# Hybrid decoder step on one core: block transposes on VectorE with transfers for the spatial branch's v and the second half's x, and sample products in pairs

## The chip, the cores and the metric

The kernel runs on one core of one Trainium2 chip. A core has TensorE for matrix products (PE in the views, its weight loads PEld), VectorE (DVE), ScalarE (ACT), GpSimd (POOL), SyncE (SP), whose queue issues this kernel's transfers, and 16 DMA engines that carry them. The metric is the time of one execution in microseconds (us); lower is better.

## The reference, cut to what matters

The reference is one step of a one-layer decoder with two gated branches, in float32. The same weights serve a prompt of 2048 tokens and a sample group of 8 sequences with 4 tokens each; the model width is 1024.

```python
h = layernorm(x) * (1 + scale) + shift
u_a, v_a, z_a, qkv, z_b, b_raw, a_raw, ga, gb = split(h @ w_in)        # 9232 columns
# spatial branch: chunks of 128 tokens, 8 heads of 128 channels
vn = layernorm(gelu(v_a)) * lnv_g + lnv_b                                # over the channels of a token
s  = einsum('hts,bnshc->bnthc', tril(w_s), vn) + b_s
y_a = gelu(u_a) * s * silu(z_a)
# recurrent branch: short convolution of q, k, v, then the gated delta rule per head
S_t = a_t S_{t-1} + beta_t k_t (v_t - a_t S_{t-1}^T k_t)^T;  o_t = S_t^T q_t
y_b = rmsnorm(o) * silu(z_b)
m   = sigmoid(ga) * (y_a @ w_pa) + sigmoid(gb) * (y_b @ w_pb)
x_new = layernorm(ALPHA * x + gate * (m @ w_o)) * ln_g + ln_b
```

For the sample group each of the 8 sequences starts from its own 128x128 state per head, so the products with the state are 8 separate ones per head, each for 4 tokens.

## The kernel before, in words

The prompt is worked in two halves of 1024 tokens; the 32 sample tokens ride with the first half. Activations lie with channels on the partitions and tokens along the free axis. A projection (`project`) makes 128 output channels at a time, a "group": for each of 8 slices of the input channels three fp32r products of a high and a low part, over column groups of 384, 384 and 256+32 tokens in the first half and 512 and 512 in the second. A group's weights are two transfers of 256 KB into `raw` buffers (three of them), which ScalarE and VectorE split into high and low parts in one of two `TWHL` buffers (`wload`). What becomes of a product is a "sink".

The order of all instructions is not written by hand. Parts of the work are generators that name an engine, an estimated duration and what they depend on; `Sched.run` advances its own model of the engines and always emits the instruction whose modelled start (plus a priority term) is earliest. Each engine and the one DMA queue on SP then run their instructions in that fixed order. Buffers are named roles over shared units (`Rc`, `Yc`), taken with `("a", role)` and given back with `S.release`; a generator that finds none free waits.

The order of the stages in each half: the heads of the recurrent branch (q, k, v, z_b and some of ga, per head), the gb groups, the v groups of the spatial branch, its u and z groups with the gating products, the rest of ga, then `w_pa`, `w_pb` and `w_o`. In the first half, beginning with the first gb group, a background task `h_next_all` prepares the second half's input, chunk after chunk.

Three places are touched:

- `v_sink` (line 1776), first half only. The v projection leaves channels on the partitions; the layer norm of v needs tokens there. A sink applies gelu (into a buffer of role `og`, four of them), TensorE transposes each 128x128 chunk (`tp`, line 450, a product with the identity) into a PSUM bank, and ScalarE copies the bank into the token-major buffers `("vt", c)`. After the eighth group `v_norm` normalises each chunk and stores it in `d_vh`; `vh_load` brings it back per head for the gating products in `gate`. In the second half v is projected token-major (`v_tokens`) and not transposed.
- `h_next` (line 801). For each of the 8 chunks of the second half: load x, normalise, 8 transposes of 128x128 on TensorE, then the affine with `scale` and `shift` on 128x128 pieces out of PSUM, four on ScalarE and four on VectorE, and two transfers of 256 KB into `d_h`, channel-major. `h_tiles` (line 836) loads the eight 128x1024 tiles of `d_h` near the end of the first half and splits each into the `X` buffers of the second half as these come free.
- `sample_head` (line 1644), once per head in the first half. Eight products of 128x64 weights (`kx`, zero outside one sequence's tokens) with that sequence's state (128x128) accumulate in one PSUM bank. Later two products with 32 rows, 128 output channels and 512 columns (`kp` with `xe`) add the new outer products to the state. Both are plain float32, and the trace shows two TensorE instructions for each such product.

The convolution's v (`v_token`, line 1346) is already turned by VectorE in 32x32 blocks (`vtrans`, line 426) and four transfers of 128-byte runs into a DRAM scratch `d_v`, and comes back token-major.

Of the kernel before, what the change touches and what calls it, by code (L numbers as in the profile page):

```python
# [11 lines left out]
ALU = mybir.AluOpType  # L12
# [3 lines left out]
KT = 8  # L16
# [153 lines left out]
def hybrid_step_kernel(ctx: ExitStack, tc: tile.TileContext, x_prompt, x_sample, state_conv, state_ssm,  # L170
# [97 lines left out]
    role("og", [Yc(28, 1), Yc(29, 1), Yc(30, 1), Yc(31, 1)])  # L268
# [21 lines left out]
    role("hf", [Yc(2, 1), Yc(3, 1), Yc(6, 1), Yc(7, 1)])  # L290
# [55 lines left out]
    d_vh = dram("d_vh", 9 * P * D)  # L346
    d_gb = dram("d_gb", KT * P * TW)
# [174 lines left out]
    def init_small():  # L522
# [8 lines left out]
        S.signal("small", t)  # L531

# [268 lines left out]
    def h_next(c):  # L801

        yield from x_norm(1, c, "hb")
        xb, t0 = S.ev[("xn", 1, c)]
        e = 0.0
        for i in range(2):
            pb = yield ("a", "pt")
            t = t0
            for k in range(4):
                t = yield from tp(Q(pb[0], k * P, P), V(xb[0] + (4 * i + k) * P, P), dep=max(t, pb[2]))  # L810
            fb = yield ("a", "hf")
            tg = max(t, fb[2])
            for k in range(4):
                t = yield from affine(V(fb[0] + k * P, P), Q(pb[0], k * P, P), 4 * i + k, k < 2, tg)
                e = max(e, t)
            S.release(pb, e)
            t = yield from dma(DV(d_h, 4 * i * P * HALF + c * P, [HALF, P], [P * HALF, 4], [1, P]),
                               V(fb[0], [P, 4], [1, P]), dep=e)
            S.release(fb, t)
            S.signal(("hB", c, i), t + 500)  # L820
        S.release(xb, e)

    def h_next_all():
        for c in range(8):
            S.spawn(h_next(c), 2.0)
            if c:
                yield ("w", ("hB", c - 1, 1))
# [8 lines left out]
    def h_tiles(todo, role, after):  # L836
        if after is not None:
            yield ("w", after)
        while todo:
# [6 lines left out]
            for c in range(8):  # L846
                t = max(t, (yield ("w", ("hB", c, k // 4))))
            t = yield from dma(V(b[0], HALF), DV(d_h, k * P * HALF, [HALF, P], [1, HALF]), dep=max(t, b[2]))
            t = max(t, (yield ("w", ("Xfree", 1, k))))
# [794 lines left out]
    def sample_head(h):  # L1644
        me = hd(0, h)
        t = 0.0
        for s in range(3):
# [30 lines left out]
        es, npq, am, m2, us = x + 320, x + 352, x + 416, x + 448, x + 480  # L1678
# [10 lines left out]
        t = yield from act(V(am, NS, **k32), Q(pb[0], 64, NS, **k32))  # L1689
# [3 lines left out]
        t = yield from tt(V(us, NS, **k32), V(m2, NS, **k32), Q(pb[0], 128, NS, **k32), ALU.subtract)  # L1693
# [16 lines left out]
        rb = yield ("a", "Rb")  # L1710
        t = yield from stt(V(rb[0], P, **k32), Q(pb[0], 0, P, **k32), V(c_sneg + h, 1, **k32), V(vs, P, **k32),
                           ALU.mult, ALU.add, dep=max(t4, t, rb[2]))
# [3 lines left out]
        S.release(pb, max(t, t5))  # L1716
        pb = yield ("a", "pt")
        t = yield from mm(Q(pb[0], 0, P, **k32), V(us, NS, **k32), V(rb[0], P, **k32), dep=max(t, pb[2]))
        t = yield from act(V(rb[0], P, **k32), Q(pb[0], 0, P, **k32))
# [14 lines left out]
        ys = x + 448  # L1734
# [9 lines left out]
        for i in range(2):  # L1744
            xe = yield ("a", "kx")
            t1 = yield from tt(V(xe[0], [P, 4], [1, P], **k32), bc(V(rb[0], P, **k32).unsqueeze(1), [NS, 4, P]),
                               bc(V(c_sel + 4 * i, 4, **k32).unsqueeze(2), [NS, 4, P]), ALU.mult, dep=max(tx, xe[2]))
            pb = yield ("a", "pt")
            t = yield from mm(Q(pb[0], 0, 512), V(kp, P, **k32), V(xe[0], 512, **k32), dep=max(t1, pb[2]))
            S.release(xe, t)  # L1750
            a = V(sb0[0] + 512 * i, 512)
            t = yield from tt(a, a, Q(pb[0], 0, 512), ALU.add, dep=max(t, t2))
            S.release(pb, t)
# [22 lines left out]
    def v_sink(half, g):  # L1776
        def sink(cgi, pb, t):
# [5 lines left out]
            cs = chunks(half, cgi)  # L1783
            ta = 0.0
            for c in cs + ([8] if ns_ else []):
                if (half, c) not in vtok and g == 0:
                    vtok[half, c] = None
                    vtok[half, c] = yield ("a", ("vt", c))
                    S.signal(("vt", half, c), vtok[half, c][2])
                ta = max(ta, (yield ("w", ("vt", half, c))))  # L1790
# [525 lines left out]
```

## Time and profile before

| what | us |
|---|---|
| three runs | 2719.08, 2724.36, 2723.06 |
| median | 2723.06 |
| the profiled execution | 2721.62 |
| its span, first to last instruction | 2719.9 |
| TensorE busy in it | 2676.6 |
| VectorE busy | 1467.0 |
| ScalarE busy | 1002.8 |
| GpSimd busy | 557.0 |

The span is what the trace covers; the execution's own time is 1.7 us more. The mean granted TensorE clock was 0.997 of the full one. Matmuls overlap in the pipeline, so the time that one costs is read from the starts of its neighbours and not from its own duration.

### The profile page before, as it was taken

To read this page: it belongs to the slowest core of one execution; us is meant where nothing else is said; L and a number is where in the kernel's file an instruction comes from. 1 tells how busy PE (TensorE), PEld (TensorE's weight loads), DVE (VectorE), ACT (ScalarE), POOL (GpSimd) and SP (SyncE) were. 2 spreads that over 40 slices of the span, in tenths; PEclk is the share of its full clock that TensorE was granted. 3 is DMA by queue.
4 is the path that set the end of the run, shared out by engine and by line. 5 is a ranking of instruction groups with operands and counts; after the bars stand their busy time and mean duration, and the time that the engine had idled before them with its cause. 6 is when DMAs were issued, how large, how long until landed. Compare 5 with 4: busy or idle time off the path is not lost.

```text
span 2719.9 us, 44021 instructions
## 1 busy us (share of the span) xinstructions
PE 2676.6 (98%) x16386; PEld 2351.3 (86%) x16386; DVE 1467.0 (54%) x3234; ACT 1002.8 (37%) x2710; POOL 557.0 (20%) x1452
## 2 busy tenths in 40 slices
PE   6999999999999999999999999999999999999998
PEld 3989999999899999999997888888888888888876
DVE  5677667777652353433547666666662323433446
ACT  5544444545343222221224535344542312222120
POOL 2044544324400000000000443433351000000001
PEclk9999999999999999999999999999999999999999
DMA  6232333223463232332433333333332422233332
GB/s 214 68 95 78 90 105 91 72 70 101 141 211 95 64 115 76 94 105 91 140 109 101 96 97 81 85 93 78 84 86 83 125 99 76 72 112 104 108 121 85
DMA packets 445618, 272.70 MB, mean 100 GB/s; under 512 B 141530, under 2 KB 411154, under 8 KB 445403
## 3 DMA queue, kind: packets, MB, share of 16 engines
q1 hardware_dynamic: 445402, 269.89, 34.6%
q8 instruction: 128, 2.10, 0.3%
q14 instruction: 88, 0.71, 0.1%
HBM read 205.70 MB, written 64.10 MB: 99 GB/s over the span
## 4 chain that ended last, share of the span: by engine, by line
PE 95%; DMA 2%; DVE 1%; ACT 1%; issue 0%; SPq 0%; POOL 0%; POOLq 0%; ACTq 0%; DVEq 0%
PE psum L447 90%; PE psum L452 3%; DMA arena<-in_w_o_dram 0%; ACT arena L398 0%; DMA arena<-in_w_in_dram 0%; PE psum L1483 0%; PE psum L1509 0%; PE psum L1520 0%; DVE arena L730 0%; DMA arena<-in_state_ssm_dram 0%; DVE arena L732 0%; PE psum L1489 0%; DVE arena L423 0%; PE psum L650 0%; DMA Y0F<-in_x_prompt_dram 0%
## 5 line engine op out<-in xcount | busy, mean ns | idle before, releaser
L447 PE MATMUL psum<-TX,TWHL 128*128 128x384 f32 (+3 forms) x9296 | 1973.4, 360 | 3.8 <-DVE TX L407 3.4
L447 PEld LDWEIGHTS psum<-TX,TWHL 128*128 128x128 f32 (+1 forms) x9296 | 1554.6, 188 | 164.0 <-issue 10.6
L398 ACT ACTIVATE arena<-psum 128x128 bf16<-128x128 f32 (+10 forms) x920 | 311.8, 348 | 769.9 <-PE psum L447 587.9
L436 POOL TENSOR_TENSOR arena<-arena 128x4 f32<-128x4 f32 (+4 forms) x139 | 120.1, 865 | 1598.3 <-DVE arena L417 1388.7
L423 DVE SCALAR_TENSOR_TENSOR arena<-arena 128x512 f32<-128x512 f32 (+8 forms) x625 | 345.8, 563 | 95.3 <-ACT arena L398 84.9
L410 POOL TENSOR_TENSOR arena<-arena 128x60 f32<-128x60 f32 (+24 forms) x992 | 358.6, 361 | 169.6 <-DMA d_v<-arena 57.5
L407 DVE TENSOR_TENSOR TWHL<-arena,TWHL 128x512 fp32r<-128x512 f32 (+1 forms) x344 | 233.1, 685 | 240.9 <-ACT TWHL L398 238.7
L423 DVE SCALAR_TENSOR_TENSOR arena<-arena,psum 128x128 f32<-128x128 f32 (+3 forms) x342 | 132.2, 403 | 360.3 <-PE psum L447 249.9
L398 ACT ACTIVATE TWHL<-arena 128x512 fp32r<-128x512 f32 x344 | 214.3, 627 | 219.1 <-PE psum L447 103.4
L398 ACT ACTIVATE arena<-arena 128x128 f32<-128x128 f32 (+9 forms) x509 | 229.4, 486 | 118.2 <-DVE arena L423 81.8
L407 DVE TENSOR_TENSOR arena<-arena 128x1024 f32<-128x1024 f32 (+13 forms) x259 | 114.3, 446 | 15.0 <-DMA arena<-in_lnv_g_dram 4.9
L447 PE MATMUL psum<-arena 128*128 128x128 f32 (+8 forms) x524 | 102.3, 293 | 1.2 <-ACT arena L398 1.0
L452 PE MATMUL psum<-arena 128*128 128x128 f32 (+7 forms) x381 | 93.2, 269 | 3.4 <-ACT TX L398 1.5
L423 DVE SCALAR_TENSOR_TENSOR arena<-psum,arena 128x512 f32<-128x512 f32 (+4 forms) x80 | 39.8, 509 | 103.8 <-PE psum L447 103.8
L447 PEld LDWEIGHTS psum<-arena 128*128 128x128 f32 (+5 forms) x524 | 73.7, 162 | 22.9 <-issue 11.2
L1228 POOL COPY arena<-arena 128x3 f32<-128x3 f32 x120 | 34.7, 289 | 267.7 <-ACT arena L398 266.8
L398 ACT ACTIVATE TX<-arena 128x512 fp32r<-128x512 f32 (+2 forms) x84 | 47.3, 587 | 93.6 <-DMA arena<-d_yb 74.2
L398 ACT ACTIVATE Y7F<-psum 32x256 f32<-32x256 f32 (+6 forms) x115 | 46.6, 405 | 86.0 <-PE psum L447 38.4
L398 ACT ACTIVATION_READ_ACCUMULATOR arena<-psum 128x1 f32 x392 | 76.6, 195 | 0.0
L452 PEld LDWEIGHTS psum<-arena 128*128 128x128 f32 (+7 forms) x381 | 49.9, 136 | 23.0 <-issue 11.9
L407 DVE TENSOR_TENSOR TX<-arena,TX 128x512 fp32r<-128x512 f32 (+2 forms) x84 | 52.4, 639 | 26.3 <-ACT TX L398 25.7
L417 DVE TENSOR_SCALAR arena<-arena 128x3 f32<-128x3 f32 (+10 forms) x234 | 47.8, 209 | 34.0 <-ACT arena L398 25.8
(244 smaller groups left out, 2733.6 us busy)
## 6 DMA issues: line engine op xcount, KB each, us to landing
arena<-in_w_in_dram SPq DMA_DIRECT2D x288, 256.0 KB
out_dram<-arena SPq DMA_DIRECT2D x25, 512.0 KB
arena<-in_x_prompt_dram SPq DMA_DIRECT2D x24, 512.0 KB
arena<-d_gc SPq DMA_DIRECT2D x16, 512.0 KB
arena<-d_blk SPq DMA_DIRECT2D x64, 128.0 KB
d_yb<-arena SPq DMA_DIRECT2D x32, 256.0 KB
d_vh<-arena SPq DMA_DIRECT2D x16, 512.0 KB
arena<-d_vh SPq DMA_DIRECT2D x16, 512.0 KB
```

The lines of the kernel that those rows point to most:

```text
L398: nc.scalar.activation(out, in_, func, **kw)
L407: nc.vector.tensor_tensor(out=out, in0=a, in1=b, op=op)
L410: nc.gpsimd.tensor_tensor(out=out, in0=a, in1=b, op=op)
L417: nc.vector.tensor_scalar(out=out, in0=a, scalar1=s1, scalar2=s2, op0=op0, **kw)
L423: nc.vector.scalar_tensor_tensor(out=out, in0=a, scalar=s, in1=b, op0=op0, op1=op1)
L436: nc.gpsimd.tensor_tensor(out=out, in0=a, in1=e, op=ALU.pow)
L447: nc.tensor.matmul(out, lhsT, rhs, start=start, stop=stop)
L452: nc.tensor.transpose(out, in_, ident[: in_.shape[0], : in_.shape[0]] if idn is None else idn)
L1228: nc.gpsimd.tensor_copy(V(c_tail + gi, [24, 3]), V(x0 + n0, 3))
```

## The change

**v of the first half.** `v_sink` applies gelu as before, then VectorE transposes the buffer in 32x32 blocks (`vtrans`) into a buffer of a new role `ogt`, and four transfers of 128-byte runs (one for each 32 partitions) write it token-major into a new DRAM scratch `d_vt`. `og` and `ogt` have two buffers each, where `og` had four. After the eighth group a new `v_load` brings each chunk back in one transfer (512 KB, or 128 KB for the 32 sample tokens) and then `v_norm` runs as before.

**x of the second half.** `h_next` transposes a normalised chunk with one `vtrans` of 128x1024 and writes it with four transfers of 128-byte runs into `d_h`, without the affine. The affine moves to `h_tiles`, on each loaded 128x1024 tile, alternately on ScalarE and VectorE, ahead of the wait for the `X` buffer.

**Sample products in pairs.** The eight `kx` products go alternately to output partitions 0 to 63 and 64 to 127, issued as one block; ScalarE copies the upper half out and VectorE adds the two. The two `kp` products use rows 0 to 31 and 32 to 63 of the array, write two PSUM banks and are issued as one block; for that `kp` is copied to partitions 32 to 63, `us` is written twice side by side so that one product fills 64 partitions, and the selector `c_sel` is copied once (`init_sel`). Some small buffers move within the head's scratch.

The diff, cut to its core:

```diff
-    role("og", [Yc(28, 1), Yc(29, 1), Yc(30, 1), Yc(31, 1)])
+    role("og", [Yc(28, 1), Yc(29, 1)])
+    role("ogt", [Yc(30, 1), Yc(31, 1)])
-    role("hf", [Yc(2, 1), Yc(3, 1), Yc(6, 1), Yc(7, 1)])
+    role("hf", [Yc(2, 2), Yc(6, 2)])
+    d_vt = dram("d_vt", 9 * P * D)
...
     def h_next(c):
         yield from x_norm(1, c, "hb")
-        xb, t0 = S.ev[("xn", 1, c)]
-        e = 0.0
-        for i in range(2):
-            pb = yield ("a", "pt")
-            t = t0
-            for k in range(4):
-                t = yield from tp(Q(pb[0], k * P, P), V(xb[0] + (4 * i + k) * P, P), dep=max(t, pb[2]))
-            fb = yield ("a", "hf")
-            tg = max(t, fb[2])
-            for k in range(4):
-                t = yield from affine(V(fb[0] + k * P, P), Q(pb[0], k * P, P), 4 * i + k, k < 2, tg)
-                e = max(e, t)
-            S.release(pb, e)
-            t = yield from dma(DV(d_h, 4 * i * P * HALF + c * P, [HALF, P], [P * HALF, 4], [1, P]),
-                               V(fb[0], [P, 4], [1, P]), dep=e)
-            S.release(fb, t)
-            S.signal(("hB", c, i), t + 500)
-        S.release(xb, e)
+        xb, t = S.ev[("xn", 1, c)]
+        fb = yield ("a", "hf")
+        t = yield from vtrans(V(fb[0], D), V(xb[0], D), dep=max(t, fb[2]))
+        S.release(xb, t)
+        for i in range(4):
+            t = yield from dma(DV(d_h, c * P + 32 * i, [HALF, 32], [32 * HALF, 32], [1, 32]),
+                               V(fb[0], [32, 32], [1, 32], p0=32 * i, np_=32), dep=t)
+        S.release(fb, t)
+        S.signal(("hB", c), t + 500)
...
     def h_tiles(todo, role, after):
             t = yield from dma(V(b[0], HALF), DV(d_h, k * P * HALF, [HALF, P], [1, HALF]), dep=max(t, b[2]))
+            t = yield from affine(V(b[0], HALF), V(b[0], HALF), k, k % 2 == 0, t)
             t = max(t, (yield ("w", ("Xfree", 1, k))))
...
     def sample_head(h):
+        t = yield from ts(V(kp, P, p0=32, np_=32), V(kp, P, **k32), 1.0, ALU.mult, dep=t)
...
         pb = yield ("a", "pt")
-        t4 = 0.0
+        t4 = yield ("o", "PE", 4 * 230.0, max(t3, td, pb[2]))
         for b in range(NB):
-            t4 = yield from mm(Q(pb[0], 0, P, np_=64), V(kx + 64 * b, 64), V(sb0[0] + b * P, P),
-                               start=b == 0, stop=b == NB - 1, dep=max(t3, td, pb[2]))
+            nc.tensor.matmul(Q(pb[0], 0, P, p0=64 * (b % 2), np_=64), V(kx + 64 * b, 64), V(sb0[0] + b * P, P),
+                             start=b < 2, stop=b >= NB - 2)
...
-        t5 = yield from act(V(osb[0], P, **q32), Q(pb[0], 0, P, **q32), dep=max(t4, osb[2]))
+        t4 = yield from act(o64, Q(pb[0], 0, P, p0=64, np_=64), dep=max(t4, osb[2]))
+        t4 = yield from tt(o64, Q(pb[0], 0, P, np_=64), o64, ALU.add)
...
-        for i in range(2):
-            xe = yield ("a", "kx")
-            t1 = yield from tt(V(xe[0], [P, 4], [1, P], **k32), bc(V(rb[0], P, **k32).unsqueeze(1), [NS, 4, P]),
-                               bc(V(c_sel + 4 * i, 4, **k32).unsqueeze(2), [NS, 4, P]), ALU.mult, dep=max(tx, xe[2]))
-            pb = yield ("a", "pt")
-            t = yield from mm(Q(pb[0], 0, 512), V(kp, P, **k32), V(xe[0], 512, **k32), dep=max(t1, pb[2]))
+        xe = yield ("a", "kx")
+        t1 = yield from tt(V(xe[0], [P, 4], [1, P], np_=64), bc(V(rb[0], P, np_=64).unsqueeze(1), [64, 4, P]),
+                           bc(V(c_sel, 4, np_=64).unsqueeze(2), [64, 4, P]), ALU.mult, dep=max(tx, xe[2]))
+        pb = yield ("a", "pt")
+        pc = yield ("a", "pu")
+        t = yield ("o", "PE", 900.0, max(t1, pb[2], pc[2]))
+        for i, q in enumerate((pb, pc)):
+            rows = dict(p0=32 * i, np_=32)
+            nc.tensor.matmul(Q(q[0], 0, 512), V(kp, P, **rows), V(xe[0], 512, **rows), start=True, stop=True)
...
     def v_sink(half, g):
-            pt = yield ("a", "pt")
-            for i, c in enumerate(cs):
-                t = yield from tp(Q(pt[0], i * P, P), V(b[0] + i * P, P), dep=max(t, pt[2]))
-            if ns_:
-                t = yield from tp(Q(pt[0], 384, P, np_=NS), V(b[0] + n0, NS), dep=max(t, pt[2]))
+            bt = yield ("a", "ogt")
+            t = yield from vtrans(V(bt[0], n), V(b[0], n), dep=max(t, bt[2]))
             S.release(b, t)
-            m = len(cs)
-            t = yield from act(V(RO + 2 * cs[0] * UNIT + g * P, [2 * UNIT, m], [1, P]),
-                               Q(pt[0], 0, [P, m], [1, P]), dep=max(t, ta))
-            if ns_:
-                t = yield from act(V(RO + 16 * UNIT + g * P, P, np_=NS), Q(pt[0], 384, P, np_=NS), dep=t)
-            S.release(pt, t)
-            S.signal(("vt", half, g, cgi), t)
+            for i in range(4):
+                t = yield from dma(DV(d_vt, c0 * D + g * P + 32 * i, [D, 32], [32 * D, n // 32], [1, 32]),
+                                   V(bt[0], [32, n // 32], [1, 32], p0=32 * i, np_=32), dep=t)
+            S.release(bt, t)
+            S.signal(("vt", half, g, cgi), t + 500)
...
+    def v_load(half, c, cgi):
+        t = 0.0
+        for g in range(KT):
+            t = max(t, (yield ("w", ("vt", half, g, cgi))))
+        n = NS if c == 8 else P
+        t = max(t, (yield ("w", ("vt", half, c))))
+        t = yield from dma(V(vtok[half, c][0], D, np_=n), DV(d_vt, c * P * D, [D, n], [1, D]), dep=t)
+        for g in range(KT):
+            S.signal(("vt", half, g, ("t", c)), t)
+        S.spawn(v_norm(half, c, ("t", c)), 1)
```

## Rows read from the trace of the kernel before

**Rows 1.** The page: busy time by engine; TensorE's busy tenths in 40 slices
```profile
PE 2676.6 (98%) x16386; PEld 2351.3 (86%) x16386; DVE 1467.0 (54%) x3234; ACT 1002.8 (37%) x2710; POOL 557.0 (20%) x1452
...
PE   6999999999999999999999999999999999999998
```
**Rows 2.** The page: the chain that ended last, shares of the span by engine
```profile
PE 95%; DMA 2%; DVE 1%; ACT 1%; issue 0%; SPq 0%; POOL 0%; POOLq 0%; ACTq 0%; DVEq 0%
```
**Rows 3.** Waits of TensorE, whole span: us in total, times, longest us
```profile
PE psum L447 <- DVE TX L407: 4.3, 3, 2.5
```
**Rows 4.** Windows: start:end, length, busy us by engine, PEclk, DMA share, GB/s
```profile
690.00:858.00 168.00, 166.47 (x1121) 146.86 (x1120) 83.19 (x197) 69.98 (x164) 27.25 (x66) 1.00 0.57 171
858.00:942.00 84.00, 84.00 (x544) 82.34 (x543) 14.78 (x28) 25.49 (x58) 1.10 (x2) 1.00 0.13 35
942.00:978.00 36.00, 36.00 (x230) 35.72 (x229) 24.77 (x50) 8.96 (x19) 4.57 (x7) 1.00 0.69 221
```
**Rows 5.** Timeline of TensorE in the v groups: start us, us, instruction, count
```profile
869.63 1.40 PE L447 MATMUL psum<-TX,TWHL 128*128 128x384 f32 x7
870.86 0.27 PE L452 MATMUL psum<-arena,Y7F 128*128 128x128 f32 x1
870.89 0.77 PE L447 MATMUL psum<-TX,TWHL 128*128 128x384 f32 x3
871.50 0.27 PE L452 MATMUL psum<-arena,Y7F 128*128 128x128 f32 x1
```
**Rows 6.** Lines by form, TensorE, 700 to 966 us: count, busy, mean ns
```profile
L452 PE MATMUL psum<-arena,Y7F 128*128 128x128 f32 x64 | 17.4, 271 | 0.0
L452 PE MATMUL psum<-arena,Y0F 128*128 128x128 f32 x48 | 13.3, 277 | 0.8 <-ACT Y0F L398 0.8
...
L452 PE MATMUL psum<-arena,Y1F 128*128 128x128 f32 x16 | 4.3, 271 | 0.0
L452 PE MATMUL psum<-arena,Y7F 128*32 128x128 f32 x8 | 2.2, 271 | 0.0
```
**Rows 7.** Timeline of TensorE: one head's kx products and what follows
```profile
306.37 1.96 PE L447 MATMUL psum<-arena 128*64 128x128 f32 x16
308.26 0.96 PE L447 MATMUL psum<-TX,TWHL 128*128 128x384 f32 x4
```
**Rows 8.** Timeline of TensorE: the last head's kx products, first and last rows
```profile
725.46 0.65 PE L447 MATMUL psum<-arena 128*64 128x128 f32 x4
...
728.16 0.40 PE L447 MATMUL psum<-TX,TWHL 128*128 128x288 f32 x1
```
**Rows 9.** Timeline of TensorE: one of a head's two kp products and what follows
```profile
326.74 1.12 PE L447 MATMUL psum<-arena 32*128 32x512 f32 x2
327.79 1.45 PE L447 MATMUL psum<-TX,TWHL 128*128 128x384 f32 x7
```
**Rows 10.** Timeline of TensorE: adaLN products in four column blocks
```profile
33.32 1.06 PE L650 MATMUL psum<-Y4F,Y7F 128*32 128x512 f32 x8
34.32 0.66 PE L452 MATMUL psum<-arena 128*128 128x128 f32 x4
```
**Rows 11.** Lines by form, VectorE, whole span
```profile
L417 DVE TENSOR_SCALAR arena<-arena 128x1024 f32<-128x1024 f32 x16 | 12.9, 805 | 5.7 <-POOL arena L436 5.7
...
L429 DVE STREAM_TRANSPOSE arena<-arena 128x384 f32<-128x384 f32 x16 | 9.1, 569 | 0.0
```
**Rows 12.** Lines by form, ScalarE, whole span
```profile
L398 ACT ACTIVATE arena<-arena 128x1024 f32<-128x1024 f32 x24 | 26.3, 1108 | 9.2 <-DVE arena L423 8.9 <-DMA Y1F<-in_w_ada_dram 0.3
```
**Rows 13.** Timeline of SP's queue: transfers of the convolution's v, and weights
```profile
677.75 3.98 SPq L381 DMA_DIRECT2D d_v<-arena  x6
...
866.11 13.92 SPq L381 DMA_DIRECT2D arena<-in_w_in_dram  x4
```
**Rows 14.** Windows: one microsecond in which those v transfers run
```profile
681.00:682.00 1.00, 1.00 (x7) 0.68 (x7) 0.85 (x2) 0.66 (x2) 0.77 (x4) 1.00 0.56 96
```
**Rows 15.** Timeline of ScalarE: the split of the weights that were issued at 866.11
```profile
877.37 0.62 ACT L398 ACTIVATE TWHL<-arena 128x512 fp32r<-128x512 f32 x1
```

More of the change, by code (lines that the diff above doesn't have):

```diff
@@ L531, in init_small, with init_sel @@
         S.signal("small", t)
+    def init_sel():
+        t = yield ("w", ("ada", 0))
+        yield from ts(V(c_sel, 4, p0=32, np_=32), V(c_sel + 4, 4, np_=NS), 1.0, ALU.mult, dep=t)
     def init_vec():
@@ L826, in h_next_all @@
             if c:
-                yield ("w", ("hB", c - 1, 1))
+                yield ("w", ("hB", c - 1))
     def h_load():
@@ L1688, in sample_head @@
         t = yield from tp(Q(pb[0], 64, NS, **k32), V(npq, NS, **k32))
-        t = yield from act(V(am, NS, **k32), Q(pb[0], 64, NS, **k32))
+        t = yield from act(V(am, NS, **k32), Q(pb[0], 64, NS, **k32), dep=max(t, t2))
         t = yield from mm(Q(pb[0], 96, NS, **k32), V(am, NS, **k32), V(npq, NS, **k32))
@@ L1692, in sample_head @@
         t = yield from mm(Q(pb[0], 128, NS, **k32), V(am, NS, **k32), V(m2, NS, **k32))
-        t = yield from tt(V(us, NS, **k32), V(m2, NS, **k32), Q(pb[0], 128, NS, **k32), ALU.subtract)
+        t = yield from tt(V(us, [NS, 2], [1, NS], **k32), bc(V(m2, NS, **k32).unsqueeze(1), [NS, 2, NS]),
+                          bc(Q(pb[0], 128, NS, **k32).unsqueeze(1), [NS, 2, NS]), ALU.subtract)
         S.release(pb, t)
@@ L1782, in sink @@
             S.release(pb, t)
[L1783 to L1790, printed above, removed]
-            pt = yield ("a", "pt")
-            for i, c in enumerate(cs):
-                t = yield from tp(Q(pt[0], i * P, P), V(b[0] + i * P, P), dep=max(t, pt[2]))
@@ L1794, in sink @@
-            if ns_:
-                t = yield from tp(Q(pt[0], 384, P, np_=NS), V(b[0] + n0, NS), dep=max(t, pt[2]))
-            S.release(b, t)
-            m = len(cs)
-            t = yield from act(V(RO + 2 * cs[0] * UNIT + g * P, [2 * UNIT, m], [1, P]),
-                               Q(pt[0], 0, [P, m], [1, P]), dep=max(t, ta))
-            if ns_:
-                t = yield from act(V(RO + 16 * UNIT + g * P, P, np_=NS), Q(pt[0], 384, P, np_=NS), dep=t)
-            S.release(pt, t)
-            S.signal(("vt", half, g, cgi), t)
+            if g == 0:
+                for c in chunks(half, cgi) + ([8] if ns_ else []):
+                    S.spawn(v_take0(half, c), 0.9)
@@ L1804, in sink @@
+            bt = yield ("a", "ogt")
+            t = yield from vtrans(V(bt[0], n), V(b[0], n), dep=max(t, bt[2]))
+            S.release(b, t)
+            for i in range(4):
[3 more added lines that the diff above has]
+            S.signal(("vt", half, g, cgi), t + 500)
             if g == KT - 1:
-                for c in cs + ([8] if ns_ else []):
-                    S.spawn(v_norm(half, c, cgi), 1)
@@ L1807, in v_sink, with v_take0 @@
-        return sink
+                for c in chunks(half, cgi) + ([8] if ns_ else []):
+                    S.spawn(v_load(half, c, cgi), 1)
+        return sink
+    def v_take0(half, c):
+        vtok[half, c] = yield ("a", ("vt", c))
+        S.signal(("vt", half, c), vtok[half, c][2])
+    def v_load(half, c, cgi):
[8 more added lines that the diff above has]
+        S.spawn(v_norm(half, c, ("t", c)), 1)
@@ L2269, in hybrid_step_kernel @@
         S.spawn(init_vec(), 1.015)
+        S.spawn(init_sel(), 1.6)
         start()
```

28 lines of the change are left out of this document (16 added, 12 removed).

## The prediction

> **What bounds the kernel now.** The page comes first: TensorE is busy for 98% of the span, and but for the first slice every slice of it is full [rows 1]. A pipelined TensorE can look busier than it is, so the chain that ended last is read next: 95% of the span leads back through TensorE, 2% through transfers, 1% each through VectorE and ScalarE [rows 2]. The list of TensorE's waits confirms it: after the start-up its largest wait is for the split of the second half's X, 4.3 us in three places, the longest 2.5 us [rows 3]. The stages that the change touches look the same: in the first half's v groups (858 to 942 us) TensorE is busy for all 84 us, VectorE for 15, ScalarE for 25, the DMA engines for 13% [rows 4]. So an instruction that leaves TensorE's queue shortens the kernel by what it costs in that queue, as long as nothing that replaces it makes TensorE wait. What moves to VectorE, ScalarE or the DMA engines is free up to that point.
>
> **Transposes that leave TensorE.** The trace of the v groups has lone transposes between products of 384 columns. Seven such products start at 869.63 and the next instruction at 870.86: 1.23 / 7 = 0.176 us each. From one transpose to the next, with three products between, it is 871.50 - 870.86 = 0.64 us; 0.64 - 3 x 0.176 = 0.11 us is what one transpose costs [rows 5]; its own 271 ns are latency. There are 64 of 128x128 and 8 of the sample tokens in the v groups (Y7F), and 48 + 16 = 64 in the preparation of the second half's x (Y0F, Y1F) [rows 6]. 136 x 0.11 = 15.0 us. The narrow eight I price like the others. A v group without its transposes is 24 products over 384, 384 and 288 columns, by the same spacing 24 x (0.176 + 0.176 + 0.132) = 11.6 us; eight take 93 us.
>
> **What takes their place.** In the v groups 24 block transposes of 384, 384 and 288 columns on VectorE at up to 569 ns [rows 11], some 12.5 us, go into these 93 us, of which VectorE works one part in six [rows 4]; ScalarE loses as many evictions. For x it is 8 of 1024 columns, by the same rate about 1.4 us each, spread over more than 100 us. Both are covered by idle time of VectorE; without that cover they would cost 24 us. The transfers grow: 4 per sink make 96, for 4.33 MB in 33,800 runs of 128 bytes. The convolution's v already leaves in such runs: six issues took 3.98 us of SP's queue [rows 13], and the core moved 96 GB/s while they ran [rows 14]. At that rate 4.33 MB take 45 us, and 96 issues at 0.66 us take 64 us of SP, in 93 us that have 13% of other traffic, 12 us [rows 4]. It fits. Behind a transfer that waits for VectorE stand the weight loads of the next group. The loads issued from 866.11 on are converted from 877.37 on [rows 13, 15], and they are converted as a group of 11.6 us begins, in about 2 us, for the group after it: some 11 + 9 us of slack. A transfer waits at most for the next sink, 4 us; the delay is absorbed. I take nothing, and up to 10 us as the bound where the queue backs up.
>
> After the last v group each chunk makes one more trip through DRAM (4.3 MB loaded). The DMA engines are at 69% there, at 221 GB/s [rows 4], so normalised v is ready some 20 us later. What is late next is the first gating product. But TensorE has the u and z products of four heads to do, 4 x 23 us by the same product times, before a gate must free a buffer. I take nothing, bound 5 us. The x chunks have some 500 us until they are loaded: nothing, though that stage has the DMA at 57% [rows 4].
>
> **The half boundary** is where a wait grows. Before, a loaded tile of `d_h` is split at once; now the affine stands first. The last tile (odd) pays a pass of VectorE, 0.8 us [rows 11], the one before a pass of ScalarE, 1.1 us [rows 12]. TensorE waits for just these tiles today [rows 3]. Splits and the layer norm queue behind the passes on both engines. I take 1.2 us lost; the bounds are 0.5 (the passes overlap) and 4 (each late tile pays its pass and a queue place).
>
> **The kx products.** An undisturbed head takes 308.26 - 306.37 = 1.89 us for 16 instructions [rows 7]. With column halves working side by side 0.95 us remain: 8 x 0.94 = 7.5 us. That column blocks do run side by side is shown by the adaLN products, eight instructions of 512 columns in 34.32 - 33.32 = 1.0 us [rows 10], where two take 1.05 us in one block [rows 9]. Also, the products are now issued as one block. The last head's took 728.16 - 725.46 = 2.70 us, with two transposes in between [rows 8]; less 1.89 and 2 x 0.11 that leaves 0.59, 0.3 us for each interruption. The eight heads' 128 instructions lie in 14 stretches, so six interruptions go: 1.8 us. Together 9.3 us; 1.8 if nothing overlapped.
>
> **The kp products.** One takes 327.79 - 326.74 = 1.05 us for two instructions [rows 9], and a head has two. If rows 0 to 31 and 32 to 63 work side by side, the second is free: 8 x 1.05 = 8.4 us, and 0.2 us per head as one stretch fewer (taken somewhat under the 0.3 above): 10.0 us. If they don't, 1.6 us. No row shows two row blocks that share their output columns; the nearest is the column blocks' overlap [rows 10], and I take the overlap. The Trainium skill (TensorEngine Tiling (Array Packing), Tiling Modes) says that tiles operate independently and that different ones can run their matmuls in parallel, row tiles of 32 x 128 among them. By that the term is the 10.0 us; no run here shows it yet. The additional copies and sums in the head are on VectorE and ScalarE, and the head's chain is filled in between projections, so they cost nothing here.
>
> **Sum.** 15.0 + 9.3 + 10.0 - 1.2 = 33.1 us. The profiled execution took 2721.6 us (span 2719.9), 1.4 below the median of the three runs, 2723.06. 2721.6 - 33.1 = 2688.5; I say 2689.
>
> **Rivals.** *Row blocks don't overlap* (17%): 8.4 us of the gain are missing, 2697. For it: no row shows the pair; against it: the column blocks.
>
> *A supply stall* (13%): weights stuck behind the small transfers, the late v, or a longer boundary cost 5 to 20 us in all, 2694 to 2709, say 2701. For it: the DMA share of 0.57 and 0.69 at both ends of the v groups, and `og` with half the buffers. Against it: no transfer holds TensorE there today [rows 3].
>
> *VectorE becomes the bound* (2%): the block transposes take longer than TensorE's (three take 0.33 us there, 0.57 on VectorE). Were both engines on the path, 24 us would come for 15: 2721.6 - 18.1 + 9 = 2712. Against it: VectorE's 15 of 84 us [rows 4]. The Trainium skill (VectorE: DVE Perf Modes, Rules for kernel authors) speaks for TensorE in a transpose of 128x128 where PSUM will do, and leaves VectorE the 32x32 blocks. The trace does not bear it out here, since TensorE is the full engine.
>
> *Slower* (4%): the 128-byte runs of `d_vt` lie 4 KB apart in DRAM, those of the convolution's v 512 bytes. If the wider pitch runs at well under half the rate, the two `ogt` buffers stay taken, gelu waits, the product banks fill and TensorE stops. It decides where the v groups' traffic reaches 93 + 33 us: (126 - 12) / 45 = 2.5 times the measured time per run. At three times it is 45 x 3 + 12 = 147 us in a stage of 93, 54 lost for 33 won: 2743. For it: nothing shown; against it: the x stores have the same pitch with 512-byte runs and hold nobody up.
>
> *No change* (2%): the order that the planner writes anew brings new waits that eat all of it.
>
> **How the numbers follow.** My forecast has the remaining 62%. Its own range is 2689 with 5 to either side: 1 us for the boundary's lower bound, some for the narrow transposes and the planner's other order, 3 for its upper. For 8 in 10 the range takes in the row blocks' rival and the near part of the stall: 2682 to 2703. Above lie the far stall, VectorE as the bound, no change and slower. A measurement here tells 0.2%, 5.4 us: faster 0.94, same 0.02, slower 0.04.
>
> **What would show it.** In the new profile TensorE has 136 instructions fewer (16,250), all of them transposes. The v groups show only products of one group, about 1 us shorter per group. The kx block is one stretch of about 1 us per head; the kp block four instructions in about 1.05 us if the row blocks overlap, 2.1 if not. At the half boundary the wait for X is 1 to 2 us longer. The prediction is wrong if TensorE shows waits for transfers or for gelu in the v groups or after them, if the paired stretches are as long as before, or if the boundary's wait grows beyond 8 us.

## The result and the profile after

| | median us | runs | of the kernel before, with 95% interval |
|---|---|---|---|
| before, same chip | 2722.14 | 4 | |
| after | 2692.02 | 4 (2690.44 to 2695.33) | 0.9891 [0.9875, 0.9906] |

The kernel became 1.1% faster: 2692.0 us against 2689 forecast, inside the range of 2682 to 2703. The two profiled executions, on which the sum was made, took 2721.62 and 2690.44 us: 31.2 us less, where 33.1 were forecast. That small miss hides two losses and some gains that the sum did not have, so the terms are gone through one by one. (Line numbers of the kernel after are a little larger: products L449, TensorE's transposes L454, activations L400, `tt` L409, block transposes L431, transfers L383.)

The page of the kernel after: busy time by engine, TensorE's 40 slices.
```profile
PE 2641.5 (98%) x16250; PEld 2331.7 (87%) x16250; DVE 1479.2 (55%) x3247; ACT 987.0 (37%) x2650; POOL 555.9 (21%) x1452
...
PE   6999999999999999999999999999999999999998
```
TensorE has exactly the 136 instructions fewer that were forecast and is still the full engine [rows 1]. VectorE gained only 12 us of work, ScalarE lost 16.

The paired products, TensorE's timeline of one head (kp, then kx in another head):
```profile
437.53 1.13 PE L1759 MATMUL psum<-arena 32*128 32x512 f32 x4
438.58 0.49 PE L449 MATMUL psum<-arena,Y5F 128*128 128x128 f32 x2
...
468.81 1.09 PE L1710 MATMUL psum<-arena 128*64 128x128 f32 x16
469.83 0.62 PE L449 MATMUL psum<-TX,TWHL 128*128 128x384 f32 x2
```
From start to the next start, four kp instructions take 438.58 - 437.53 = 1.05 us, as long as two did [rows 9]; sixteen kx instructions take 469.83 - 468.81 = 1.02 us, where they took 1.89 [rows 7]. Each is one block without a transpose in it.

The waits of TensorE, whole span, those that are new or longer:
```profile
PE psum L449 <- DVE TX L409: 6.9, 3, 5.2
...
PE psum L449 <- ACT Y7F L400: 2.4, 1, 2.4
...
PE psum L449 <- ACT Y6F L400: 0.6, 1, 0.6
```
The wait for the second half's X grew from 4.3 [rows 3] to 6.9 us. Two waits for gelu did not exist before, that of v (`Y7F`, where `og` and `ogt` lie) and that of the first u group (`Y6F`): the supply stall of the second rival, in a small form. The windows around the first of them (us, busy by engine, granted clock, DMA share, GB/s):
```profile
835.00:850.00 15.00, 12.62 (x76) 12.33 (x76) 4.28 (x8) 3.58 (x7) 0.00 (x0) 0.99 0.49 90
850.00:870.00 20.00, 20.00 (x114) 20.00 (x113) 3.85 (x7) 3.56 (x7) 0.00 (x0) 0.92 0.49 97
870.00:890.00 20.00, 20.00 (x128) 20.00 (x127) 5.20 (x9) 4.42 (x8) 0.00 (x0) 1.00 0.40 74
```
TensorE is idle for 2.4 us of the first window; in the second it is full again but its granted clock is 0.92, and it gets through fewer products (114 against 128). A narrower window shows why:
```profile
850.00:852.00 2.00, 2.00 (x8) 2.00 (x7) 0.00 (x0) 0.00 (x0) 0.00 (x0) 0.50 0.55 83
```
Right behind the pause the clock stands at the lower of its two levels, 0.50 of the full one (1.2 of 2.4 GHz). Over the 20 us that takes 20 x (1 - 0.92) = 1.6 us more than the pause itself. In the kernel before these stages run at 1.00 [rows 4].

What holds the gelu of v shows in the timeline of ScalarE, VectorE and TensorE around the wait:
```profile
844.51 0.63 ACT L400 ACTIVATE TWHL<-arena 128x512 fp32r<-128x512 f32 x1 [6.90 <-PE psum L449]
845.18 0.69 DVE L409 TENSOR_TENSOR TWHL<-arena,TWHL 128x512 fp32r<-128x512 f32 x1 [6.75 <-ACT TWHL L400]
846.10 0.63 ACT L400 ACTIVATE TWHL<-arena 128x512 fp32r<-128x512 f32 x1 [0.95 <-PE psum L449]
846.76 0.69 DVE L409 TENSOR_TENSOR TWHL<-arena,TWHL 128x512 fp32r<-128x512 f32 x1 [0.89 <-ACT TWHL L400]
847.37 0.93 DVE L431 STREAM_TRANSPOSE Y7F<-Y7F 128x384 f32<-128x384 f32 x2
848.04 0.87 ACT L400 ACTIVATE Y7F<-psum 128x384 f32<-128x384 f32 x2 [1.31 <-DVE Y7F L431]
...
848.58 3.67 PE L449 MATMUL psum<-TX,TWHL 128*128 128x384 f32 x13 [2.38 <-ACT Y7F L400]
```
Read it backwards. TensorE needs a PSUM bank, so a gelu; the gelu needs an `og` buffer, so a block transpose; the transpose stands in VectorE's queue behind the low part of the weight split, which sat 6.75 us waiting for ScalarE's high part, which sat 6.90 us until TensorE gave up a `TWHL` buffer. Nothing here is slow. The cause is the order: weight splits that could not start yet stand ahead of the transpose.

The wait of 0.6 us comes where the v groups end and the first u group begins, and its lines differ:
```profile
912.44 0.58 DVE L431 STREAM_TRANSPOSE Y7F<-Y7F 128x384 f32<-128x384 f32 x1 [2.40 <-DMA d_vt<-Y7F]
912.64 0.49 ACT L400 ACTIVATE Y6F<-psum 128x384 f32<-128x384 f32 x1 [3.71 <-PE psum L449]
913.02 0.48 ACT L400 ACTIVATE Y7F<-psum 128x384 f32<-128x384 f32 x1
913.18 12.04 PE L449 MATMUL psum<-TX,TWHL 128*128 128x384 f32 x73 [0.58 <-ACT Y6F L400]
```
No split is in the way here. The block transpose waited 2.40 us until a store of `d_vt` had left its `ogt` buffer. So the last two gelus of v come only behind it (913.02 and 918.08). Until then their products fill two of the three PSUM banks for products, and TensorE must wait for the third, which the gelu of u empties. This wait comes from the two `ogt` buffers and their stores.

The half boundary, the same view:
```profile
1427.81 1.24 ACT L400 ACTIVATE arena<-arena 128x1024 f32<-128x1024 f32 x1 [1.76 <-DMA arena<-d_h]
...
1430.75 0.81 DVE L419 TENSOR_SCALAR arena<-arena 128x1024 f32<-128x1024 f32 x1 [0.23 <-DMA arena<-d_h]
1431.48 0.69 DVE L409 TENSOR_TENSOR TX<-arena,TX 128x512 fp32r<-128x512 f32 x1
...
1432.08 1.28 DVE L425 SCALAR_TENSOR_TENSOR arena<-arena 128x1024 f32<-128x1024 f32 x1
1432.22 1.07 PE L449 MATMUL psum<-TX,TWHL 128*40 128x512 f32 x2 [5.21 <-DVE TX L409]
1433.28 1.29 DVE L409 TENSOR_TENSOR TX<-arena,TX 128x512 fp32r<-128x512 f32 x2
1434.02 2.35 PE L449 MATMUL psum<-TX,TWHL 128*40 128x512 f32 x5 [0.72 <-DVE TX L409]
```
The affine passes (1.24 us on ScalarE, 0.81 on VectorE) stand ahead of the splits, and the low part of tile 6 (1431.48) queues behind the affine of tile 7. VectorE also has the layer norm of the first half's output in between (L425, 1.28 us). A stretch at the lower clock follows the wait here too, in both kernels: 0.62 granted over 1460 to 1465 us before, 0.50 over 1430 to 1435 us after.

Block transposes on VectorE, lines by form (count, busy us, mean ns, idle before):
```profile
L431 DVE STREAM_TRANSPOSE Y7F<-Y7F 128x384 f32<-128x384 f32 x16 | 9.1, 572 | 30.0 <-DMA d_vt<-Y7F 22.3 <-ACT Y7F L400 4.3 <-issue 3.3
L431 DVE STREAM_TRANSPOSE Y0F<-Y0F 128x1024 f32<-128x1024 f32 x6 | 7.5, 1242 | 3.5 <-ACT Y0F L400 3.2 <-DMA d_h<-Y0F 0.3
```
0.57 us as priced [rows 11], and 1.24 against the 1.4 estimated. 22.3 us of VectorE's idle time ahead of the v transposes are waits for `ogt` to leave by transfer.

### The profile page after: what moved, and what is told of

Its sections match the earlier page's. It is cut to its first block, busy times and chain, and to the rows that moved or that the text cites. A ratio compares the mean times of both kernels' runs of the same rounds, so it can differ in the third digit from the quotient of the medians.

```text
span 2688.7 us, 43893 instructions
## 1 busy us (share of the span) xinstructions
PE 2641.5 (98%) x16250; PEld 2331.7 (87%) x16250; DVE 1479.2 (55%) x3247; ACT 987.0 (37%) x2650; POOL 555.9 (21%) x1452
## 5 line engine op out<-in xcount | busy, mean ns | idle before, releaser
L449 PE MATMUL psum<-TX,TWHL 128*128 128x384 f32 (+3 forms) x9296 | 1959.4, 359 | 9.3 <-DVE TX L409 5.9
L449 PEld LDWEIGHTS psum<-TX,TWHL 128*128 128x128 f32 (+1 forms) x9296 | 1556.3, 188 | 163.8 <-DVE TX L409 7.0
L400 ACT ACTIVATE arena<-psum 128x128 bf16<-128x128 f32 (+9 forms) x888 | 299.4, 346 | 719.7 <-PE psum L449 596.8
L425 DVE SCALAR_TENSOR_TENSOR arena<-arena 128x512 f32<-128x512 f32 (+9 forms) x633 | 348.9, 560 | 91.2 <-ACT arena L400 79.6
L412 POOL TENSOR_TENSOR arena<-arena 128x60 f32<-128x60 f32 (+24 forms) x992 | 352.1, 355 | 174.7 <-DMA d_v<-arena 36.9
L409 DVE TENSOR_TENSOR TWHL<-arena,TWHL 128x512 fp32r<-128x512 f32 (+1 forms) x344 | 233.2, 687 | 198.3 <-ACT TWHL L400 196.1
L425 DVE SCALAR_TENSOR_TENSOR arena<-arena,psum 128x128 f32<-128x128 f32 (+3 forms) x342 | 132.7, 404 | 357.2 <-PE psum L449 246.6
L400 ACT ACTIVATE TWHL<-arena 128x512 fp32r<-128x512 f32 x344 | 213.6, 627 | 240.3 <-PE psum L449 117.0
L400 ACT ACTIVATE arena<-arena 128x128 f32<-128x128 f32 (+9 forms) x513 | 234.7, 493 | 130.4 <-DVE arena L425 86.2
L409 DVE TENSOR_TENSOR arena<-arena 128x1024 f32<-128x1024 f32 (+12 forms) x251 | 108.6, 438 | 9.6 <-DMA arena<-in_lnv_g_dram 5.6
L454 PE MATMUL psum<-arena 128*128 128x128 f32 (+8 forms) x381 | 93.6, 269 | 2.6 <-ACT Y3F L400 0.8
L400 ACT ACTIVATE Y7F<-psum 32x256 f32<-32x256 f32 (+6 forms) x115 | 46.5, 405 | 117.8 <-DVE Y7F L431 37.5
L425 DVE SCALAR_TENSOR_TENSOR arena<-psum,arena 128x512 f32<-128x512 f32 (+4 forms) x72 | 36.9, 528 | 84.2 <-PE psum L449 84.0
L400 ACT ACTIVATE TX<-arena 128x512 fp32r<-128x512 f32 (+2 forms) x84 | 46.9, 586 | 89.3 <-DMA arena<-d_yb 72.2
L400 ACT ACTIVATION_READ_ACCUMULATOR arena<-psum 128x1 f32 x392 | 76.5, 195 | 0.0
L419 DVE TENSOR_SCALAR arena<-arena 128x3 f32<-128x3 f32 (+8 forms) x247 | 54.4, 224 | 36.3 <-ACT arena L400 24.2
L449 PEld LDWEIGHTS psum<-arena 128*128 128x128 f32 (+3 forms) x364 | 55.2, 171 | 17.1 <-issue 7.0
L454 PEld LDWEIGHTS psum<-arena 128*128 128x128 f32 (+8 forms) x381 | 49.7, 136 | 22.8 <-issue 12.0
L449 PE MATMUL psum<-arena 128*128 128x128 f32 (+5 forms) x364 | 66.5, 269 | 1.2 <-ACT arena L400 1.0
L409 DVE TENSOR_TENSOR TX<-arena,TX 128x512 fp32r<-128x512 f32 (+2 forms) x84 | 52.1, 639 | 21.7 <-ACT TX L400 21.5
```

The costliest lines, as they stand in the source:

```text
L400: nc.scalar.activation(out, in_, func, **kw)
L409: nc.vector.tensor_tensor(out=out, in0=a, in1=b, op=op)
L412: nc.gpsimd.tensor_tensor(out=out, in0=a, in1=b, op=op)
L419: nc.vector.tensor_scalar(out=out, in0=a, scalar1=s1, scalar2=s2, op0=op0, **kw)
L425: nc.vector.scalar_tensor_tensor(out=out, in0=a, scalar=s, in1=b, op0=op0, op1=op1)
L449: nc.tensor.matmul(out, lhsT, rhs, start=start, stop=stop)
```

## The experiments

The repeat of the changed kernel, run beside those that are variants of it, gave 2693.41 us (4 runs), 0.9902 [0.9886, 0.9919], 26.7 us under its own runs of before, with the same three waits (2.38, 0.58, 5.35 + 0.72 us).

> The changed kernel once more, as the measure for the three kernels beside it: 2692 again, 29.6 us under the kernel before.

**One part alone.** Three kernels each apply one part of the diff, as it stands in the section on the change, to the kernel before: `e_v` the v of the first half, `e_x` the x of the second half with its affine, `e_pairs` the sample products.

```diff
 # e_v, against before
+    role("og", [Yc(28, 1), Yc(29, 1)])
+    role("ogt", [Yc(30, 1), Yc(31, 1)])
...
 # e_x, against before
+        t = yield from vtrans(V(fb[0], D), V(xb[0], D), dep=max(t, fb[2]))
...
+            t = yield from affine(V(b[0], HALF), V(b[0], HALF), k, k % 2 == 0, t)
...
 # e_pairs, against before
+            nc.tensor.matmul(Q(pb[0], 0, P, p0=64 * (b % 2), np_=64), V(kx + 64 * b, 64), V(sb0[0] + b * P, P),
+                             start=b < 2, stop=b >= NB - 2)
```

> The kernel before with the change of v alone; x and the sample products as before. If TensorE's queue sets the time, 72 transposes at 0.11 us make 7.9 us less. Theory A: the wait of 2.4 us that the changed kernel shows at 848 us, with the slower clock after it (1.7 us) and a second wait of 0.6 us, comes from the two ogt buffers and the order that the planner makes of them; then the wait is here too and about 3 us are left: 2719. Theory B: it comes from the x stores, whose 128-byte runs share the DMA engines with those of v; here x is stored in 512-byte runs, so there is no such wait and the kernel takes 2714.

> The kernel before with the change of x alone. 64 transposes at 0.11 us make 7.0 us less; the wait for X at the half boundary grows from 3.4 to 5.9 us as in the changed kernel: 4.5 us in all, 2717.5. Rival: the longer boundary comes from the other parts' reordering and not from the affine on the loaded tiles; then the wait stays at 3.4 us and it is 2715.

> The kernel before with the sample products in pairs alone. Theory: 9.3 us from kx and 10.0 us from kp, 19.3 us: 2703. The kx block takes about 1.0 us per head, the kp block 1.06. Rival: the longer chain of a sample head delays buffers, TensorE gets waits among the heads, and less than 14 us is left: over 2708.

| | median us (runs) | of before (2721.6) | less, us |
|---|---|---|---|
| e_v | 2712.63 (8) | 0.9971 [0.9961, 0.9982] | 9.0 |
| e_x | 2713.87 (10) | 0.9975 [0.9966, 0.9985] | 7.7 |
| e_pairs | 2701.91 (4) | 0.9933 [0.9917, 0.9950] | 19.7 |

The waits of TensorE in `e_v`:
```profile
PE psum L449 <- DVE TX L409: 4.7, 3, 2.5
...
PE psum L449 <- ACT Y6F L400: 0.6, 1, 0.6
```
The 2.4 us wait is absent, with the same two `og` and two `ogt` buffers and the same 96 transfers. So the v change does not bring it alone. The kernel after adds the 128-byte stores of x and the paired products; which of the two it takes was not separated, since no run has v with only one of them. The wait of 0.6 us is here as well. Matching each projection product of `e_v` with the same one of before, the trace gains 7.6 us from 526 to 1093 us, over the v groups and most of u and z: 72 transposes x 0.11 = 7.9, less the wait of 0.58, is 7.3. The price per transpose holds, the narrow ones included.

`e_x` carries the longer boundary, and no other new wait (timeline of TensorE):
```profile
1451.93 1.07 PE L447 MATMUL psum<-TX,TWHL 128*40 128x512 f32 x2 [5.46 <-DVE TX L407]
```
5.46 + 0.73 us, where `e_v` and `e_pairs` have 2.55 + 1.26 and 2.55 + 1.27. The boundary's loss belongs to the x change. `e_x` takes 7.7 us less all the same, where the theory had 4.5 (the interval leaves 4.1 to 9.3). Matched in the same way, its trace, of the fastest of the ten runs, gains 10.9 us from 701 to 902 us. Small waits of before that are gone make 1.5 of it; 9.4 are left for 64 transposes, 0.15 us each where 0.11 were priced. What makes them dearer was not looked into.

`e_pairs` gives 19.7 us against the 19.3 of the sum (9.3 + 10.0). Together the three make 36.4 us, the whole change 30.1 beside its own runs of before and 26.7 in the repeat. The intervals leave most of that difference open, but two parts have a place: the wait at the v groups with its clock, 2.4 + 1.6 us, which no part has alone, and about 1.5 us that the profile of each part gains ahead of 160 us, before any of the touched places is reached, and that the sum counts three times.

**Without the affine.** `e_noaff` takes the affine out of `h_tiles`.
```diff
-            t = yield from affine(V(b[0], HALF), V(b[0], HALF), k, k % 2 == 0, t)
```

> The changed kernel without the affine on the loaded tiles of the second half's x (so the second half is computed from an x without scale and shift). Theory: the waits for X at the half boundary go back from 5.9 to about 3.4 us, and the kernel takes 2.5 us less than the changed one. Rival: the tiles themselves come later, because a tile now waits for all eight chunks and for buffers; then the wait stays near 5.9 us.

One run, 2695.51 us. TensorE's timeline at the boundary:
```profile
1436.06 0.85 PE L449 MATMUL psum<-TX,TWHL 128*40 128x512 f32 x2 [2.55 <-DVE TX L409]
1437.98 9.70 PE L449 MATMUL psum<-TX,TWHL 128*40 128x512 f32 x31 [1.07 <-DVE TX L409]
```
The boundary is back at 3.6 us, close to the one before (2.55 + 0.85 = 3.4): the affine causes the difference. The 2.4 us wait at the v groups stays, since nothing there was changed. The total can't be compared, because of the start-up. The window over it, of this kernel and then of the kernel after:
```profile
20.00:60.00 40.00, 34.49 (x165) 17.86 (x160) 16.56 (x50) 23.13 (x42) 2.46 (x5) 0.70 0.63 202
```
```profile
20.00:60.00 40.00, 31.70 (x205) 19.17 (x199) 22.08 (x67) 28.98 (x56) 2.65 (x5) 0.96 0.62 202
```
The granted clock of this execution was 0.70 there, where it is 0.96 in the other, and its projections began 7.2 us later (56.33 against 49.16 us). From ahead of the boundary (1430 us) to 1573 us of the kernel before, products matched one by one, it gains 1.8 us on the kernel after.

**Four buffers.** `e_ring` gives `og` and `ogt` four buffers each.
```diff
-    role("og", [Yc(28, 1), Yc(29, 1)])
-    role("ogt", [Yc(30, 1), Yc(31, 1)])
+    role("og", [Yc(28, 1), Yc(29, 1), Yc(24, 1), Yc(25, 1)])
+    role("ogt", [Yc(30, 1), Yc(31, 1), Yc(26, 1), Yc(27, 1)])
```

> The changed kernel with four og and four ogt buffers (the ZZ buffers, which lie idle in the v groups). Theory buffers: the wait of 2.4 us at the beginning of the v groups, the one of 0.6 us and the 1.7 us of slower clock come from two ogt buffers that are still being stored; with four they go, about 4 us less than the changed kernel. Theory planner: VectorE is made to split weights ahead of the block transpose because the planner counts a run of 128 bytes as 1.7 ns and so sees its DMA engines full; more buffers let its transposes come earlier all the same, so the wait shrinks here too, but it goes as well in the kernel with the cheaper count and two buffers.

2687.09 us (4 runs, 2686.04 to 2690.52), 0.9878 [0.9863, 0.9893]: 6.3 us under the repeat on the same chip (2690.49 to 2696.06). Matched with the kernel after, its products gain 5.0 us by the end of the v groups, where about 4 were expected. The windows at the v groups:
```profile
835.00:850.00 15.00, 15.00 (x92) 14.89 (x92) 4.10 (x8) 2.44 (x5) 0.00 (x0) 1.00 0.61 108
850.00:870.00 20.00, 20.00 (x127) 20.00 (x126) 4.84 (x9) 4.39 (x10) 0.00 (x0) 1.00 0.51 101
```
TensorE is full and the clock stays at 1.00; both waits for gelu are gone. The DMA engines carry more here (0.61 against 0.49) and hold nobody up. This is the fastest version of the study.

**A cheaper count of small transfers.** The planner charges a transfer of 128-byte runs four times that of 512-byte ones, 1.7 ns a run; the traces show 1.3 (96 GB/s [rows 14], for 128 bytes), and where only stores of `d_vt` run 1.5 (83 GB/s in the window at 850 us) and 1.2 (108 GB/s in `e_v` from 931 to 933 us). `e_cost` takes 1.2 and changes only that estimate, with two buffers kept.
```diff
-        t = yield ("o", "DMA", (n * 4 / 300.0 * max(1.0, 512.0 / run), late), dep)
+        t = yield ("o", "DMA", (n * 4 / 300.0 * max(1.0, 370.0 / run), late), dep)
```

> The changed kernel with one number of the planner changed: it counts a run of 128 bytes at 2.9 times the time per byte of a long one (1.2 ns a run, as the traces show it) in place of 4. No instruction is added or removed. Theory planner: the wait at the beginning of the v groups goes or falls under 1 us, about 4 us less than the changed kernel. Theory buffers: the transfers themselves hold the two ogt buffers, whatever the planner believes; the wait of 2.4 us stays.

2693.92 us (4 runs, 2689.89 to 2697.61), 0.9900 [0.9886, 0.9915]: no gain. But the wait of 2.4 us is gone (that of 0.6 us stays). The timeline of its VectorE and ScalarE in the same groups, and a new wait of TensorE in the second half:
```profile
841.57 0.57 DVE L431 STREAM_TRANSPOSE Y7F<-Y7F 128x384 f32<-128x384 f32 x1
...
845.72 0.48 DVE L431 STREAM_TRANSPOSE Y7F<-Y7F 128x288 f32<-128x288 f32 x1 [3.58 <-issue]
...
850.58 1.39 ACT L400 ACTIVATE TWHL<-arena 128x512 fp32r<-128x512 f32 x2 [2.09 <-DMA arena<-in_w_in_dram]
851.25 0.69 DVE L409 TENSOR_TENSOR TWHL<-arena,TWHL 128x512 fp32r<-128x512 f32 x1 [5.05 <-ACT TWHL L400]
...
1972.46 1.13 PE L449 MATMUL psum<-Y1F 128*128 128x256 f32 x4 [0.62 <-DVE Y3F L425]
```
The transpose at 845.72 now stands ahead of the split at 851.25. So the wait came from the order that the overestimated transfers led to, and more buffers were one of two ways out of it. Against the kernel after, products matched one by one, this execution gains 4.1 us from 813 to 853 us (times of the kernel after), what the wait and its clock had cost. The total did not follow: from 1414 to 2058 us it loses 3.9 us, of which the wait above is one visible part. The planner wrote the rest of the order anew too; that the loss lies in the order alone was not shown. This execution also began slowly, as the one without the affine did: its granted clock was 0.70 here too, and its projections began 5.2 us later than in the kernel after.
```profile
20.00:60.00 40.00, 32.46 (x165) 20.04 (x164) 18.09 (x53) 24.79 (x45) 2.30 (x5) 0.70 0.62 201
```
How the other three runs began is not known.

**The boundary, three tries.** `e_edge` splits the affine of the last two tiles by column group: ScalarE writes the high part straight from the raw tile, and VectorE's affine comes only ahead of the low part. `e_yout` is `e_ring` in which the first half's last output chunks wait for X, so that their layer norms leave VectorE's queue free. `e_yout_edge` is `e_ring` with both.
```diff
 # e_edge, against after; k >= 6
+                    t = yield from affine(hi, a, k, True, t)
+                    t = yield from affine(a, a, k, False, t)
+                    t = yield from tt(lo, a, hi.bitcast(F32), ALU.subtract, dep=t)
...
 # e_yout, against e_ring
+        if half == 0 and c > 5:
+            yield ("w", ("X", 1, 0, KT - 1))
```

> The changed kernel with the affine of the last two tiles of x by column group: ScalarE makes the high part straight from the loaded tile with scale and shift, VectorE makes the affine in float32 and then the low part. Theory: the affine's place in the queues of both engines is what lengthens the wait at the half boundary from 3.4 to 5.9 us; per tile only 0.45 us are added here, and the wait falls to about 4.3 us: 1.5 us less than the changed kernel. Rival: VectorE's queue at the boundary (layer norms of the outputs) sets it, and the wait stays over 5 us.

> The changed kernel with four og and four ogt buffers, and with the layer norms of the first half's last three output chunks held back until the last tile of the second half's x is split. Theory: it is VectorE's queue, with layer norms between the affine and the low parts of the last two tiles, that keeps the waits for X at the half boundary at 5.8 us; with the norms behind the tiles the waits fall by about 1.5 us, to about 4.3 us, and the kernel takes 2685.5, against 2687.1 with the buffers alone. Rival: the transfers of the last tiles set the waits; then they stay over 5.3 us.

> As the kernel with the held-back layer norms, and with the affine of the last two tiles by column group as in the run of that name. Theory VectorE's queue: without norms between, the shorter chain per tile now counts: the waits fall to about 4.0 us, 2685. Rival transfers: they stay over 5.3 us.

| | median us (4 runs each) | of before | boundary waits, us |
|---|---|---|---|
| e_edge | 2693.37 | 0.9898 [0.9883, 0.9913] | 4.38 + 1.53 |
| e_yout | 2690.41 | 0.9883 [0.9866, 0.9899] | 4.93 |
| e_yout_edge | 2693.13 | 0.9893 [0.9878, 0.9907] | 2.38 + 2.97 |

In `e_edge` the theory failed: 5.9 us, as in the kernel after. `e_yout` missed its forecast too (4.9 us against 4.3, 2690.4 against 2685.5), and `e_yout_edge` lies with its rival (5.35 us, 2693.1 against 2685). The VectorE timeline of `e_edge` shows what came instead:
```profile
1432.50 0.55 DVE L419 TENSOR_SCALAR arena<-arena 128x512 f32<-128x512 f32 x1 [0.26 <-ACT TX L400]
1432.96 1.28 DVE L425 SCALAR_TENSOR_TENSOR arena<-arena 128x1024 f32<-128x1024 f32 x1
1434.15 0.69 DVE L409 TENSOR_TENSOR TX<-arena,TX 128x512 fp32r<-128x512 f32 x1
```
Between the last affine piece and its low part stands a layer norm of 1.28 us. `e_yout` takes the norms away, and its VectorE then stands before the affine, idle, waiting for the tile itself; a wait of TensorE for another engine's product appears 540 us later:
```profile
1427.51 0.81 DVE L419 TENSOR_SCALAR arena<-arena 128x1024 f32<-128x1024 f32 x1 [2.84 <-DMA arena<-d_h]
...
1965.86 1.13 PE L449 MATMUL psum<-Y1F 128*128 128x256 f32 x4 [1.87 <-DVE Y3F L425]
```
The low part of tile 6, for which TensorE waits, stands right behind this affine of tile 7 (1428.24), as in the kernel after; so the load of tile 7 counts through that order. That the order alone holds TensorE is argued and not shown: without the affine the same loads gave 3.6 us, but no version has the low part of tile 6 ahead of the affine of tile 7. Against `e_ring` (4.95 + 0.82) the two tries with held-back norms take at most 0.8 us off the waits, and `e_yout` as a whole is no faster than `e_ring` (0.9883 against 0.9878 of before): products matched one by one, it gains 2.4 us from 1251 to 1551 us of `e_ring` and loses 5.3 us from there to 2253 us, in the second half's heads.

## Why the prediction was right, point by point

**Transposes, 15.0 us: right.** All 136 left, and `e_v` shows the price of 0.11 us in the v groups, 7.6 us with a wait of 0.58 inside. Those of x gave more in `e_x`, 9.4 us for the 7.0 of the sum. VectorE's time was covered, and no stage shows it as the bound, so that rival is out.

**kx, 9.3 us: right.** 8 x (1.89 - 1.02) = 7.0 and, at the prediction's own price, 1.8 for the six interruptions, 8.8 us. The 1.8 was not measured by itself.

**kp, 10.0 us: right.** The step with no row behind it was the overlap of row blocks. The pair takes 1.05 us, as one product did. That agrees with the Trainium skill (TensorEngine Tiling (Array Packing), Tiling Modes), by which different tiles can run their matmuls in parallel. The largest rival (17%) is out. `e_pairs` confirms both terms together, 19.7 against 19.3.

**The transfers, nothing: the step that was mis-sized.** The prediction named waits for gelu in the v groups or after them as a sign of being wrong, and two came. The bound of up to 10 us "where the queue backs up" held, but the place was another than argued. No wait of TensorE there leads to a weight load, and the wider pitch did no harm. SP's queue in the kernel before (`d_v`, runs 512 bytes apart) and in the kernel after (`d_vt`, 4 KB apart):
```profile
679.72 2.01 SPq L381 DMA_DIRECT2D d_v<-arena  x4
```
```profile
848.84 3.00 SPq L383 DMA_DIRECT2D d_vt<-Y7F  x6
```
Both take 0.50 us an issue; the 0.66 of the prediction has a pause in it. While they run the core moves 96 GB/s at a DMA share of 0.56 [rows 14] and 83 at 0.55 (the window at 850 us), so the slower rival is out too. What was overlooked is a fixed order on VectorE. The prediction put the transposes into idle time, by busy share, and did not ask what stands ahead of them in the queue. A split that waits for TensorE ahead of a transpose for which TensorE waits cost 2.4 us, and the lower clock behind it 1.6; a transpose that waits for its `ogt` buffer cost 0.6: 4.6 us. `e_v`, `e_ring` and `e_cost` settle the cause of the first as far as they go: it comes with two buffers, the planner's dear count and more of the change than v alone, and either more buffers or the cheaper count removes the 2.4. The 0.6 goes with more buffers only.

**The late v, nothing: right.** No wait of TensorE follows the v groups for it.

**The boundary, 1.2 us: too small.** The waits grew by 6.9 - 4.3 = 2.6 us, inside the bounds of 0.5 to 4 but over the 1 to 2 us that the prediction expected to see. `e_noaff` shows the affine as the cause; the sum took one tile's pass, while the low part of the tile before queues behind it as well, and VectorE's norms stand between.

**What the sum lacked on the other side.** 15.0 + 8.8 + 10.0 - 4.6 - 2.6 = 26.6, and 31.2 were measured between the two profiles. The kernel after is 0.9 us ahead from its first projections on (51 us), and two waits of before, 0.52 us at 761 and 0.63 at 802, are gone; 0.6 us more came between 109 and 157 us, in `e_v` too. That makes 2.7 us, and some 2 us are not assigned. The products, matched one by one, say where they are: the lead over the kernel before is 31.8 us just ahead of the boundary, 30.0 at 1573 us of the kernel before and 31.1 from 2060 us on. The boundary thus took nearer 1.8 us than 2.6, and the second half's heads, whose code the change leaves alone, gave 1.1 back. Why is open, and executions of one kernel differ by more (2690.4 to 2695.3 for the one after). The two losses, 7.2 us in all, are of the size that the rival of a supply stall named (5 to 20 us); without the small gains the time would have been at its near end, about 2694. That 2689 came within 3 us of the median is thus in part luck, the cancelling of small terms; each of the three large ones was right by itself, within 2.4 us.

## What to carry to other kernels

Where one engine is full all the time, price an instruction by what it adds between its neighbours' starts (0.11 us), not by its own duration (0.27 us); in the v groups that price held when the instructions left. When work moves to an engine with idle time, look at what will stand ahead of it in that engine's fixed order, above all an instruction that itself waits for the full engine; a second pair of buffers was worth more here (5.0 us in the v groups) than any repair of the order. Where a planner writes the order, judge a small edit by the whole run and not by the wait that it removes: `e_cost` removed its wait and `e_yout` shortened the boundary, and both lost the time again in the second half's heads. And look at how an execution begins before its total is used: two of the profiled ones started 5 and 7 us late at a granted clock of 0.70.

## What the runs showed of the hardware

A pause of 2.4 us of a TensorE that had been full was followed by a stretch at the lower of its two clock levels (0.50 granted over 850 to 852 us), so the pause cost 1.6 us more than itself; the windows around the wait of 0.6 us (910 to 914 and 914 to 920 us) show 1.00. Two products on rows 0 to 31 and 32 to 63 with the same output columns in different PSUM banks, in plain float32 and so two instructions each, ran in the time of one (1.05 us). Stores of 128-byte runs left SP's queue at 0.50 us an issue, at a pitch of 4 KB in DRAM as at 512 bytes.
